# A two-layer mixture-of-experts transformer on one core: keys projected in two halves, with the first half's hats of two chunks traced between them

## The chip, the cores and the metric

One Trainium2 chip, of which the kernel uses one core. The metric is the device time of one launch in microseconds (us), the median over runs. A profiled execution of the kernel before gives the rows below; its own time stands beside the median in the table.

## What is computed

256 latent and 256 context tokens of width 1024 go through two layers, all in fp32. Layer 0 has attention, layer 1 an RWKV-7 mixer; a mixture of 16 experts follows each. The change touches the RWKV mixer alone (16 heads of 64, two scan directions d):

```python
mix = lambda j: h + xx * x_mix[j]
r, k, v = heads(mix(0) @ w_r), heads(mix(2) @ w_k), heads(mix(3) @ w_v)
g = jax.nn.sigmoid(mix(5) @ g1) @ g2
kk = k * heads(k_k)
kk = kk * lax.rsqrt(jnp.maximum(jnp.sum(kk * kk, axis=-1, keepdims=True), 1e-24))
for d in range(2):
    decay = ...   # from mix(1), two small matrices
    iclr = jax.nn.sigmoid(heads(a0[d] + (mix(4) @ a1[d]) @ a2[d]))
    k_d = k * (1.0 + (iclr - 1.0) * heads(k_a))
    ins = (r, decay, k_d, v, -kk, kk * iclr)
    s_ctx, y_c = wkv_scan(zero, *(t[:, :L] for t in ins), reverse=d == 1)
    _, y_l = wkv_scan(s_ctx, *(t[:, L:] for t in ins), reverse=d == 1)
    y = y + jnp.concatenate([y_c, y_l], axis=1)
o = groupnorm(y) + bonus * v
yl = (o * g)[:, L:] @ w_o
```

## The kernel before

One program without branches. Layer 0, then layer 1's mixer (about 980 to 1405 us of the profiled span), its output projection and router, and then layer 1's experts, whose weights stream from HBM. A list scheduler decides at build time in which order the instructions stand on each engine, from the order in which the program traces them, its dependences and its costs; on the chip each engine takes its instructions in that order. Matrix multiplies of the projections run as three fp32r passes on a high and a low part (`mm3`, L148 to L150), for which ScalarE copies the high part of a weight tile (L142) and VectorE, or GpSimd for some, subtracts the low one (L143).

`rwkv` traces the steps of a list, one letter each (L1236): `l` the small matrices of decay and iclr (`loras`), `K` the keys, `R` the receptances, `gate`, `V` the values, `H0` to `H3` the hats of four chunks of 128 tokens, `S0` to `S3` their triangular solves, `c0` to `c7` the sequential scan over pieces of 64 tokens, `M4` to `M7` the outputs.

**Keys.** `proj_k` (L1388) works in four rounds n of 256 columns, four heads each. After each, `k_sink` (L1398) takes the accumulators out as kr and k1 (ScalarE, VectorE), squares kr on GpSimd (L1408), sums the squares by head with TensorE (L1410), raises them to the power -1/2 on GpSimd (`rn`, L1415), transposes the result on TensorE (L1419), copies it to `rT` (VectorE), spreads it over 128 partitions by a product with the constant e4 on TensorE (L1424, fp32), multiplies kr by it (VectorE, L1425) and stores kr and k1 in DRAM (`kks`, issued on ScalarE's queue, L1427). kr and k1 have four buffers each, and the outputs of `R` (`ro`, L1440) and of `V` use the same buffers, as does the gate's sigmoid `gs` (L1543).

**Hats.** `wkv_hat` (L1554) works on pieces: chunk u, direction d, half kh of the heads, 16 pieces in all, four per chunk. A piece loads kk (L1572, from `kks`), sig and icl (L1577, L1579) by SP's queue, multiplies sig by a triangle on TensorE (L1585), takes exponentials on ScalarE (Ep, Em, L1588, L1589), makes A (VectorE, L1594), kk times icl (VectorE, L1608) and BK (GpSimd, L1618), then multiplies them by head in eight small matmuls on TensorE (L1624), four into each of two PSUM tiles, and copies the results to AB on ScalarE (L1630, four copies). 

**Solves.** `wkv_solve` takes the four pieces of a chunk: it begins with a transpose of AB on VectorE (L1651), 62 steps of two VectorE operations (L1658, L1660), and a transpose back (L1662). The scan `c` multiplies the state Z on TensorE and updates it on VectorE (L1837, L1838).

Of the kernel before, what the change touches and what calls it, by code (L numbers as in the profile page):

```python
# [9 lines left out]
F32 = mybir.dt.float32  # L10
# [18 lines left out]
def shape_constants():  # L29
    c = {}  # L30
# [30 lines left out]
    c["gmk"] = np.where(np.arange(128)[:, None] < 64, lt[:, None] > t, lt[:, None] < t)  # L61
    c["e4"] = (i == np.arange(256)[None, :] // 64)
    c["hsel"] = (i // 64 == np.arange(2)[None, :])
# [16 lines left out]
class Net:  # L80
# [1107 lines left out]
    def rwkv(self, st, se, sf):  # L1188
# [46 lines left out]
        self.trit = "k"  # L1235
        for o in ["l", "K", "h", "H0", "R", "H1", "Vm", "gate", "V", "hx", "close", "S0", "H2", "S1", "c0", "H3", "x", "S2", "c1", "S3", "c2", "c3", "M4", "n", "c4", "M5", "c5", "M6", "c6", "M7", "c7", "F"]:  # L1236
            u = int(o[1]) if len(o) == 2 and o[1].isdigit() else None
            if o == "h":
# [19 lines left out]
            elif o == "l":  # L1258
                self.loras(lo, h)
            elif o == "K":  # L1260
                self.proj_k(h)
            elif o == "R":
# [9 lines left out]
            elif o[0] == "H":  # L1272
                q = int("0011"[u])
                self.AB.append(vp[q].tile([128, 2, 16, 64], F32, tag="AB", bufs=2 if q == 0 else 2, name=self.uid("AB")))
                self.wkv_hat(u, self.AB[-1])
            elif o[0] == "S":
# [110 lines left out]

    def proj_k(self, h):  # L1388
        mh, ml = self.mix_split(2, h)
        for n in range(4):  # L1390
            acc = [self.ps(tag="L") for _ in range(2)]
            for k, wh, wl in self.wsplit("rwkv_w_k", n, 256):
                for q in range(2):
                    qs = slice(q * 128, q * 128 + 128)
                    self.mm3(acc[q], wh[:, qs], wl[:, qs], mh[k], ml[k], k == 0, k == KT - 1)
            self.k_sink(n, acc)

    def k_sink(self, n, acc):  # L1398
# [19 lines left out]
        for t in range(4):  # L1418
            nc.tensor.transpose(pt[:, t * 128:(t + 1) * 128], rn[:, t, :], self.ident)  # L1419
        rT = self.lp.tile([4, 512], F32, tag="rT", bufs=2, name=self.uid("rT"))  # L1420
        nc.vector.tensor_copy(rT, pt)
        for i, ts in enumerate(out):
            pb = self.ps(tag="k")
            nc.tensor.matmul(pb, self.cst("e4")[0:4, i * 128:i * 128 + 128], rT, start=True, stop=True)  # L1424
            nc.vector.tensor_tensor(out=ts[0], in0=ts[0], in1=pb, op=ALU.mult)  # L1425
# [127 lines left out]

    def wkv_hat(self, u, AB):  # L1554
        nc = self.nc
        CD = float(np.exp(np.float32(-0.5)))
        lat = u >= 2
        for d in range(2):
# [8 lines left out]
            fm = self.fm[d, u]  # L1567
            for kh in range(2):
                wk = self.hp[(2 * d + kh) % len(self.hp)]
# [49 lines left out]
                nc.sync.dma_start(out=self.hB[d, u][:, :, ks, :], in_=BK)  # L1619
                for lc in range(2):  # L1620
                    p = self.ps((128, 4, 128), tag="G")
                    q64 = slice(64 * d, 64 * d + 64)
                    for q in range(4):
                        nc.tensor.matmul(p[q64, q, :], BK[:, lc, q, Bs] if d == 0 else A[:, lc, q, :],  # L1624
                                         Abd[:, lc, q].rearrange("p a t -> p (a t)"),
                                         start=True, stop=True, skip_group_check=True)
                    pq = p.rearrange("p q (a t) -> p (q a) t", a=2)
                    for jb in range(2):
                        rows = slice(64 * d + 32 * jb, 64 * d + 32 * jb + 32)
                        nc.scalar.activation(AB[rows, lc, 8 * kh:8 * kh + 8, 0:64 - 32 * jb],  # L1630
                                             pq[rows, :, 32 * jb:64], AF.Copy)
                if lat:
# [486 lines left out]
```

## Time and profile before

| | us |
|---|---|
| runs, median of 3 | 1976.08 (1969.65 to 1979.23) |
| the profiled execution, its own time | 1968.82 |
| its span | 1967.0 |
| PE (TensorE) busy in the span | 1703.4 (87%) |
| DVE (VectorE) busy | 972.1 (49%) |
| ACT (ScalarE) busy | 729.0 (37%) |
| POOL (GpSimd) busy | 321.9 (16%) |
| mean granted TensorE clock | 0.936 of 2.4 GHz |

The shares are averages over stages with different limits, so they don't tell what a change in one stage is worth. The rows that matter are those of the stage that the change touches, 1055 to 1410 us, and of the end of the program.

### The profile page before, as it was taken

The numbers are of one execution on the slowest core, as the hardware profiler recorded it, in microseconds if no ns is written. First come the engines' busy times: TensorE is split into PE (matmuls) and PEld (weight loads), VectorE is DVE, ScalarE is ACT, GpSimd is POOL, SyncE is SP. The second block draws the span as 40 slices with busy tenths as digits, with TensorE's granted clock in tenths as the row PEclk, the third lists the DMA queues.
The fourth block names the chain that finished last, engine by engine and source line by source line (L and its number), as shares of the span: only waits on it lengthen the run. The fifth ranks groups of instructions, "written<-read, shape, count | busy, mean of one in ns | idle before, by whom it ended". The sixth has DMA issues, their size and how long they took to land. (4 is left out here: it accounts for less than half of the span.)

```text
span 1967.0 us, 30330 instructions
## 1 busy us (share of the span) xinstructions
PE 1703.4 (87%) x11673; PEld 1037.8 (53%) x11673; DVE 972.1 (49%) x1864; ACT 729.0 (37%) x1379; POOL 321.9 (16%) x313
## 2 busy tenths in 40 slices
PE   5978997889999999994898978889777999988986
PEld 3845565645555555552577767879653333322321
DVE  2466555756555555657745589973653111110101
ACT  2324543545444554543545765642141000100000
POOL 2040032000000000014557353510330000000000
PEclk7989998899999999997898987889988999999999
DMA  8377766699999999995357878635395999999996
GB/s 335 108 295 255 264 186 236 224 356 410 409 410 410 407 409 365 378 361 150 108 186 226 274 209 239 197 102 125 120 392 225 409 409 409 410 408 409 409 409 274
DMA packets 232019, 585.95 MB, mean 298 GB/s; under 512 B 43131, under 2 KB 87443, under 8 KB 231862
## 3 DMA queue, kind: packets, MB, share of 16 engines
q1 hardware_dynamic: 213446, 545.46, 75.2%
q10 hardware_dynamic: 15536, 27.92, 3.9%
q0 software_dynamic: 2880, 10.49, 1.5%
q8 instruction: 96, 1.57, 0.3%
q14 instruction: 61, 0.50, 0.1%
HBM read 544.19 MB, written 39.63 MB: 297 GB/s over the span
## 5 line engine op out<-in xcount | busy, mean ns | idle before, releaser
L143 DVE TENSOR_TENSOR lo<-raw,hi 128x512 fp32r<-128x512 f32 x456 | 305.2, 713 | 208.3 <-ACT hi L142 203.1
L142 ACT ACTIVATE hi<-raw 128x512 fp32r<-128x512 f32 x488 | 292.3, 628 | 215.2 <-PE ps L150 148.1
L1122 PE MATMUL ps<-raw,XT 128*64 128x512 f32 x1024 | 233.5, 597 | 15.3 <-DMA raw<-in_moe_w_dram 15.3
L1122 PEld LDWEIGHTS ps<-raw,XT 128*64 128x64 f32 x1024 | 72.2, 136 | 170.2 <-issue 125.6
L1128 DVE TENSOR_TENSOR h<-h,ps 128x512 f32<-128x512 f32 x16 | 11.0, 688 | 303.9 <-PE ps L1122 303.9
L1140 PE MATMUL ps<-raw,hT 128*64 128x512 f32 x512 | 120.2, 607 | 15.9 <-DVE hT L1133 9.4
L1986 PE MATMUL ps<-raw,XT 128*64 128x512 f32 x512 | 122.7, 600 | 0.0
L148 PE MATMUL ps<-hi,xh 128*128 128x512 f32 x256 | 100.8, 417 | 19.6 <-ACT hi L142 15.6
L149 PE MATMUL ps<-lo,xh 128*128 128x512 f32 x256 | 106.1, 414 | 0.3
L150 PE MATMUL ps<-hi,xl 128*128 128x512 f32 x256 | 102.5, 401 | 0.0
L259 POOL TENSOR_TENSOR rs<-rs,mh 128x2 f32<-128x2 f32 (+2 forms) x5 | 3.9, 772 | 533.9 <-DVE rs L258 533.9
L1140 PEld LDWEIGHTS ps<-raw,hT 128*64 128x64 f32 x512 | 35.2, 138 | 80.4 <-issue 55.2
L1932 POOL DMA_INDIRECT G<-rowbuf,ix x12 | 13.2, 1100 | 392.7 <-DVE oh L1953 261.3
L148 PEld LDWEIGHTS ps<-hi,xh 128*128 128x128 f32 x256 | 49.5, 195 | 48.1 <-ACT hi L142 21.5
L227 PE MATMUL ps<-raw,cv 128*32 128x256 f32 x768 | 61.5, 421 | 9.1 <-DMA raw<-in_ada_w_dram 5.5
L1986 PEld LDWEIGHTS ps<-raw,XT 128*64 128x64 f32 x512 | 34.0, 136 | 64.0 <-issue 61.5
L149 PEld LDWEIGHTS ps<-lo,xh 128*128 128x128 f32 x256 | 49.9, 195 | 24.7 <-DVE lo L143 7.6
L1127 ACT ACTIVATE h<-ps 128x512 f32<-128x512 f32 x16 | 9.6, 597 | 143.0 <-PE ps L1122 143.0
L1144 ACT ACTIVATE ye<-ps 128x512 f32<-128x512 f32 x16 | 9.6, 597 | 141.7 <-PE ps L1140 141.7
L1986 PE MATMUL ps<-raw,hT 128*64 128x512 f32 x256 | 61.3, 600 | 0.8 <-DVE hT L2059 0.8
L148 PE MATMUL ps<-hi,th 128*128 128x512 f32 x128 | 50.0, 407 | 6.2 <-ACT hi L142 6.1
L150 PEld LDWEIGHTS ps<-hi,xl 128*128 128x128 f32 x256 | 49.9, 195 | 9.4
(484 smaller groups left out, 3456.0 us busy)
## 6 DMA issues: line engine op xcount, KB each, us to landing
raw<-in_moe_w_dram SPq DMA_DIRECT2D x384, 1024.0 KB
raw<-in_ada_w_dram SPq DMA_DIRECT2D x48, 1024.0 KB
kk<-kks SPq DMA_DIRECT2D x16, 512.0 KB
hB<-BK SPq DMA_DIRECT2D x16, 512.0 KB
BKm<-hB SPq DMA_DIRECT2D x16, 512.0 KB
raw<-in_attn_w_in_dram SPq DMA_DIRECT2D x6, 1024.0 KB
raw<-in_attn_w_out_dram SPq DMA_DIRECT2D x8, 512.0 KB
ybuf<-ye ACTq DMA_DIRECT2D x8, 512.0 KB
```

The lines of the kernel that those rows point to most:

```text
L142: nc.scalar.activation(hi, src, AF.Copy)
L143: (lo_eng or nc.vector).tensor_tensor(out=lo, in0=src, in1=hi.bitcast(F32), op=ALU.subtract)
L148: mm(out, lh, rh, start=start, stop=False, skip_group_check=True)
L149: mm(out, lh, rl, start=False, stop=False, skip_group_check=True)
L150: mm(out, ll, rh, start=False, stop=stop, skip_group_check=True)
L227: nc.tensor.matmul(p[32 * q:32 * q + 32, :], self.cv[:, k, :], w[:, a, q * 256:(q + 1) * 256], start=(k == 0), stop=(k == KT - 1), skip_gr ...
L1122: nc.tensor.matmul(acc[64 * n:64 * n + 64, :], XT[:, k, e % 4 * 64:e % 4 * 64 + 64], w[:, a, n * 512:(n + 1) * 512], start=(k == 0), stop= ...
L1127: nc.scalar.activation(h, hs[0], AF.Silu)
L1128: nc.vector.tensor_tensor(out=h, in0=h, in1=hs[1], op=ALU.mult)
L1140: nc.tensor.matmul(acc[64 * n:64 * n + 64, :], hT[:, k % 4, (k // 4) * 64:(k // 4) * 64 + 64], w[:, a, n * 512:(n + 1) * 512], start=(k == ...
L1932: nc.gpsimd.indirect_dma_start(out=G, out_offset=None, in_=self.rowbuf[:, :], in_offset=bass.IndirectOffsetOnAxis(ap=idx[:, 0:1], axis=0))
L1986: nc.tensor.matmul(acc[0][64 * n:64 * n + 64, :], lhs(k), w[:, a, ns], start=(k == 0), stop=(k == KT - 1), skip_group_check=True)
```

## The change

Three parts. (1) The list has `K0`, the first two key rounds (heads 0 to 7), then `H00` and `H10`, the first head half of chunks 0 and 1, then `K1`, the last two rounds, then `H01`, `R` and `H11`. Before, `K` stood whole, then `H0`, `R`, `H1`. The solves take whole chunks in both. (2) In `k_sink`, rT is split into a high part (ScalarE copy) and a low part (VectorE subtraction) in one fp32r tile of 36 partitions, and the product with e4 is one fp32r pass of both in place of an fp32 product. (3) In `wkv_hat`, the eight small matmuls of a piece go to one PSUM tile, alternately to its lower and upper 64 partitions.

```diff
@@ -59,7 +59,7 @@
     t = np.arange(64)[None, :]
     c["gm0"], c["gm1"] = lt[:, None] <= t, lt[:, None] >= t
     c["gmk"] = np.where(np.arange(128)[:, None] < 64, lt[:, None] > t, lt[:, None] < t)
-    c["e4"] = (i == np.arange(256)[None, :] // 64)
+    c["e4"] = (i % 32 == np.arange(256)[None, :] // 64) * (i < 64)
     c["hsel"] = (i // 64 == np.arange(2)[None, :])
     late = ("tri0", "tri1", "gm0", "gm1", "gmk", "hsel", "e4")
     off, parts = {}, [[], [], []]
@@ -1233,8 +1233,8 @@
         lo = self.pool(slo, "loras", side="right")
         self.Z, self.main, self.y2, self.late, wk = [None, None], {}, [], [], None
         self.trit = "k"
-        for o in ["l", "K", "h", "H0", "R", "H1", "Vm", "gate", "V", "hx", "close", "S0", "H2", "S1", "c0", "H3", "x", "S2", "c1", "S3", "c2", "c3", "M4", "n", "c4", "M5", "c5", "M6", "c6", "M7", "c7", "F"]:
-            u = int(o[1]) if len(o) == 2 and o[1].isdigit() else None
+        for o in ["l", "K0", "h", "H00", "H10", "K1", "H01", "R", "H11", "Vm", "gate", "V", "hx", "close", "S0", "H2", "S1", "c0", "H3", "x", "S2", "c1", "S3", "c2", "c3", "M4", "n", "c4", "M5", "c5", "M6", "c6", "M7", "c7", "F"]:
+            u = int(o[1]) if o[1:].isdigit() else None
             if o == "h":
                 slo.close()
                 vp.append(self.pool(ssv, "solve", side="right"))
@@ -1257,8 +1257,8 @@
                 self.hat_tiles("A", wk)
             elif o == "l":
                 self.loras(lo, h)
-            elif o == "K":
-                self.proj_k(h)
+            elif o[0] == "K":
+                self.proj_k(h, (2 * u, 2 * u + 1))
             elif o == "R":
                 self.proj_r(h)
             elif o == "V":
@@ -1271,8 +1271,9 @@
                 self.gate_hidden(h)
             elif o[0] == "H":
                 q = int("0011"[u])
-                self.AB.append(vp[q].tile([128, 2, 16, 64], F32, tag="AB", bufs=2 if q == 0 else 2, name=self.uid("AB")))
-                self.wkv_hat(u, self.AB[-1])
+                if u == len(self.AB):
+                    self.AB.append(vp[q].tile([128, 2, 16, 64], F32, tag="AB", bufs=2, name=self.uid("AB")))
+                self.wkv_hat(u, self.AB[u], (0, 1) if len(o) == 2 else (int(o[2]),))
             elif o[0] == "S":
                 self.wkv_solve(vp[int("0101"[u])], u, self.AB[u])
             elif o == "x":
@@ -1385,9 +1386,21 @@
                     ws = slice(b * width, (b + 1) * width)
                     yield m * c + a + b, wh[:, ws], wl[:, ws]
 
-    def proj_k(self, h):
-        mh, ml = self.mix_split(2, h)
-        for n in range(4):
+    def proj_k(self, h, ns):
+        if ns[0]:
+            return self.proj_k_part(ns)
+        nc = self.nc
+        self.mk = self.mix_split(2, h)
+        self.e4 = self.lp.tile([36, 256], F32R, name="e4r")
+        nc.scalar.activation(self.e4, self.cst("e4")[0:36, :], AF.Copy)
+        self.rT = [self.lp.tile([36, 512], F32R, name=f"rT{i}") for i in range(2)]
+        for t in self.rT:
+            nc.gpsimd.memset(t.bitcast(F32), 0.0)
+        self.proj_k_part(ns)
+
+    def proj_k_part(self, ns):
+        mh, ml = self.mk
+        for n in ns:
             acc = [self.ps(tag="L") for _ in range(2)]
             for k, wh, wl in self.wsplit("rwkv_w_k", n, 256):
                 for q in range(2):
@@ -1417,11 +1430,12 @@
         pt = self.ps((4, 512), tag="k")
         for t in range(4):
             nc.tensor.transpose(pt[:, t * 128:(t + 1) * 128], rn[:, t, :], self.ident)
-        rT = self.lp.tile([4, 512], F32, tag="rT", bufs=2, name=self.uid("rT"))
-        nc.vector.tensor_copy(rT, pt)
+        rT = self.rT[n % 2]
+        nc.scalar.activation(rT[0:4, :], pt, AF.Copy)
+        nc.vector.tensor_tensor(out=rT[32:36, :], in0=pt, in1=rT[0:4, :].bitcast(F32), op=ALU.subtract)
         for i, ts in enumerate(out):
             pb = self.ps(tag="k")
-            nc.tensor.matmul(pb, self.cst("e4")[0:4, i * 128:i * 128 + 128], rT, start=True, stop=True)
+            nc.tensor.matmul(pb, self.e4[:, i * 128:i * 128 + 128], rT, start=True, stop=True)
             nc.vector.tensor_tensor(out=ts[0], in0=ts[0], in1=pb, op=ALU.mult)
             for a, t in enumerate(ts):
                 nc.scalar.dma_start(out=self.kks[:, a, 2 * n + i], in_=t.rearrange("p (v t) -> p v t", v=2))
@@ -1551,7 +1565,7 @@
     Bs = {0: slice(0, 64), 1: slice(64, 128)}
     Ks = {0: slice(64, 128), 1: slice(0, 64)}
 
-    def wkv_hat(self, u, AB):
+    def wkv_hat(self, u, AB, khs):
         nc = self.nc
         CD = float(np.exp(np.float32(-0.5)))
         lat = u >= 2
@@ -1565,7 +1579,7 @@
             mid, end = (0, 64) if d == 0 else (64, 0)
             v4 = lambda t: t.rearrange("p k (c t) -> p k c t", c=2)
             fm = self.fm[d, u]
-            for kh in range(2):
+            for kh in khs:
                 wk = self.hp[(2 * d + kh) % len(self.hp)]
                 ks = slice(4 * kh, 4 * kh + 4)
                 kk = self.ht(wk, "kk", [128, 2, 4, 128])
@@ -1617,18 +1631,18 @@
                 nc.vector.tensor_tensor(out=kd, in0=kd, in1=icl, op=ALU.mult)
                 nc.gpsimd.tensor_tensor(out=bk(Ks), in0=v4(kd), in1=Em[:, :, :, inc], op=ALU.mult)
                 nc.sync.dma_start(out=self.hB[d, u][:, :, ks, :], in_=BK)
-                for lc in range(2):
-                    p = self.ps((128, 4, 128), tag="G")
-                    q64 = slice(64 * d, 64 * d + 64)
-                    for q in range(4):
-                        nc.tensor.matmul(p[q64, q, :], BK[:, lc, q, Bs] if d == 0 else A[:, lc, q, :],
+                p = self.ps((128, 4, 128), tag="G")
+                for q in range(4):
+                    for lc in range(2):
+                        nc.tensor.matmul(p[64 * lc:64 * lc + 64, q, :], BK[:, lc, q, Bs] if d == 0 else A[:, lc, q, :],
                                          Abd[:, lc, q].rearrange("p a t -> p (a t)"),
                                          start=True, stop=True, skip_group_check=True)
-                    pq = p.rearrange("p q (a t) -> p (q a) t", a=2)
+                pq = p.rearrange("p q (a t) -> p (q a) t", a=2)
+                for lc in range(2):
                     for jb in range(2):
                         rows = slice(64 * d + 32 * jb, 64 * d + 32 * jb + 32)
                         nc.scalar.activation(AB[rows, lc, 8 * kh:8 * kh + 8, 0:64 - 32 * jb],
-                                             pq[rows, :, 32 * jb:64], AF.Copy)
+                                             pq[64 * lc + 32 * jb:64 * lc + 32 * jb + 32, :, 32 * jb:64], AF.Copy)
                 if lat:
                     nc.gpsimd.tensor_tensor(out=rr, in0=kd, in1=rr, op=ALU.mult)
                     pbn = self.ps((128, 8), tag="G")
```

Lines past `k_sink` stand 14 lower in the code after the change (L1424 is L1438 there, L1618 is L1632). Only the RWKV stage's order differs; from the tail of the scan to the end the instructions stand alike.

GpSimd's queue before, from the squares of key round 3 on (ksq), with rn2172 the power of round 2 and rn2196 that of round 3; the first hat's rows follow behind these:

```order
L1408 TENSOR_TENSOR ksq2192_9234<-kr2190_9232 128x512
L1408 TENSOR_TENSOR ksq2195_9244<-kr2193_9242 128x512
L1415 TENSOR_TENSOR rn2172_9141<-rn2172_9141,mh_66 128x16
L143 TENSOR_TENSOR lo2286_9615<-raw2282_9596,hi2285_9614 128x512
L143 TENSOR_TENSOR lo2291_9649<-raw2287_9630,hi2290_9648 128x512
L143 TENSOR_TENSOR lo2300_9691<-raw2296_9672,hi2299_9690 128x512
L1321 MEMSET Abd_9279 128x1024
L1652 MEMSET T2463_10447 128x1024
L1653 MEMSET T2463_10447 128x32
L1415 TENSOR_TENSOR rn2196_9252<-rn2196_9252,mh_66 128x16
L143 TENSOR_TENSOR lo2305_9725<-raw2301_9706,hi2304_9724 128x512
```

The same queue now, with BK2170, BK2181 and BK2191 the second to fourth hat piece's, ksq2231 and ksq2234 the squares of round 3:

```order
L1632 TENSOR_TENSOR BK2170_9137<-kk2162_9114,Em2166_9121 128x4x2x64
L1605 COPY fm01_8367<-Em2177_9170 128x4x2
L1604 COPY fm11_8371<-Ep2186_9217 128x4x2
L1632 TENSOR_TENSOR BK2181_9186<-kk2173_9163,Em2177_9170 128x4x2x64
L1605 COPY fm11_8371<-Em2187_9218 128x4x2
L1421 TENSOR_TENSOR ksq2231_9443<-kr2229_9441 128x512
L1421 TENSOR_TENSOR ksq2234_9453<-kr2232_9451 128x512
L1632 TENSOR_TENSOR BK2191_9234<-kk2183_9211,Em2187_9218 128x4x2x64
L1428 TENSOR_TENSOR rn2212_9350<-rn2212_9350,mh_66 128x16
L1428 TENSOR_TENSOR rn2235_9461<-rn2235_9461,mh_66 128x16
L143 TENSOR_TENSOR lo2404_10166<-raw2400_10147,hi2403_10165 128x512
```

Both powers stood ahead of the first hat piece; now both stand behind the fourth piece's BK.

ScalarE's queue before, around the last store of key round 3 (kr2193) and the first hat's exponentials; ro2316 is an output of R:

```order
L1427 DMA kks_8324<-kr2193_9242 128x512 [waits DMAHW0_49,DVE_49]
L1370 ACTIVATE mxh2368_10016<-mx2384_10047 128x512 [waits DVE_49,PE_49]
L142 ACTIVATE hi2408_10117<-raw2407_10115 128x512 [waits DMAHW6_49,Pool_49]
L1588 ACT_TABLE_LOAD [waits DMAHW5_49]
L1588 ACTIVATE Ep2205_9288<-ps2207_9290 128x260 [waits PE_49]
L1589 ACTIVATE Em2206_9289<-ps2207_9290 128x260
L1588 ACTIVATE Ep2205_9288<-ps2208_9295 128x260 [waits PE_49]
L1589 ACTIVATE Em2206_9289<-ps2208_9295 128x260
L142 ACTIVATE hi2410_10133<-raw2407_10115 128x512 [waits PE_49,Activation_49]
L1370 ACTIVATE mxh2369_10017<-mx2385_10051 128x512 [waits DVE_49,PE_49]
L1441 ACTIVATE ro2316_9808<-ps2294_9670 128x512 [waits PE_49]
```

ScalarE's queue now, behind the last of the early hats' copies; kr2206 and kr2209 are key round 2's, ro2305 and ro2329 outputs of R, gs2387 the gate's sigmoid, kr2229 round 3's, hi2403 and what follows weights of V:

```order
L1434 ACTIVATE rT0_8830<-ps2213_9353 4x512 [waits PE_49]
L1441 DMA kks_8324<-kr2206_9330 128x512 [waits DMAHW5_49,DVE_49]
L1441 DMA kks_8324<-kr2209_9340 128x512 [waits DMAHW6_49,DVE_49]
L1455 ACTIVATE ro2305_9763<-ps2283_9625 128x512 [waits DMAHW5_49]
L1456 DMA rsc_8331<-ro2305_9763 128x512 [waits DMAHW7_49,Activation_49]
L1455 ACTIVATE ro2329_9907<-ps2307_9769 128x512 [waits DMAHW6_49]
L1456 DMA rsc_8331<-ro2329_9907 128x512 [waits Activation_49]
L1557 ACT_TABLE_LOAD
L1557 ACTIVATE gs2387_10095<-ps2375_10057 128x160 [waits DMAHW7_49]
L1434 ACTIVATE rT1_8831<-ps2236_9464 4x512 [waits PE_49]
L142 ACTIVATE hi2403_10165<-raw2400_10147 128x512 [waits PE_49]
```

The waits on a DMAHW semaphore are for transfers. Before, round 3's store stood ahead of the first hat; now the last outputs of R, the gate's sigmoid and V's next weights stand behind round 2's stores, and ro2305 and ro2329 wait for transfers.

TensorE's queue now; ps2192 is the fourth early piece's product, ps2213 the transposes of round 2, ps2388 and ps2390 the gate's, ps2391 the first of V:

```order
L1637 MATMUL ps2192_9246<-Abd_9063,A2190_9231 64x128 x8
L1432 MATMUL ps2213_9353<-C_60,rn2212_9350 4x128 x4
L1438 MATMUL ps2214_9360<-rT0_8830,e4r_8828 128x512
L1438 MATMUL ps2215_9365<-rT0_8830,e4r_8828 128x512
L1423 MATMUL ps2228_9440<-C1_8332,ksq2231_9443 128x2 x4
L1423 MATMUL ps2228_9440<-C1_8332,ksq2234_9453 128x2 x4
L1559 MATMUL ps2388_10097<-C_60,gs2387_10095 128x128
L1560 MATMUL ps2388_10097<-C_60,gs2387_10095 32x128
L1559 MATMUL ps2390_10104<-C_60,gs2389_10102 128x128
L1560 MATMUL ps2390_10104<-C_60,gs2389_10102 32x128
L148 MATMUL ps2391_10109<-hi2396_10115,mxh2351_10009 128x512
```

Before, rounds 2 and 3's products with e4 (L1424) stood ahead of the first hat's triangle, and the gate's transposes stood between hat pieces. Now round 2's stand behind the fourth early piece, ahead of the gate and V, and round 3's transposes and e4 products (L1432, L1438) stand 21 and 41 rows behind V's first row.

## Rows read from the trace of the kernel before

**Rows 1.** The page: TensorE's busy tenths and GB/s in 40 slices of 49.2 us.
```profile
PE   5978997889999999994898978889777999988986
...
GB/s 335 108 295 255 264 186 236 224 356 410 409 410 410 407 409 365 378 361 150 108 186 226 274 209 239 197 102 125 120 392 225 409 409 409 410 408 409 409 409 274
```

**Rows 2.** The chain of waits, its first expert matmul and a late transfer: start, us, what.
```profile
1493.29 1.07 PE ps L1122 x3
...
1889.59 18.55 DMA raw<-in_moe_w_dram
```

**Rows 3.** Busy time by stage: PE, PEld, DVE, ACT, POOL, clock, DMA, rate.
```profile
971.00:975.00 4.00, 4.00 (x13) 3.09 (x12) 1.68 (x3) 0.93 (x2) 1.47 (x2) 0.57 0.42 168
1055.00:1093.00 38.00, 29.44 (x200) 25.71 (x198) 26.51 (x31) 25.74 (x52) 29.15 (x24) 0.91 0.77 240
1093.00:1154.40 61.40, 61.33 (x330) 50.12 (x328) 44.15 (x77) 42.66 (x94) 21.36 (x25) 1.00 0.79 243
1120.30:1268.90 148.60, 126.61 (x1537) 109.56 (x1536) 136.81 (x261) 104.55 (x217) 68.94 (x83) 0.83 0.78 220
```

**Rows 4.** Timeline, SP's queue: loads of the first and third hat piece.
```profile
1055.76 0.72 SPq L1577 DMA_DIRECT2D sig<-sgs  x1
...
1088.23 2.91 SPq L1572 DMA_DIRECT2D kk<-kks  x2
...
1094.21 0.42 SPq L1579 DMA_DIRECT2D icl<-ics  x1
```

**Rows 5.** Timeline, TensorE: the first triangle, a key sink's e4 product, a hat's.
```profile
1065.12 1.98 PE L1424 MATMUL ps<-rT,C 4*128 4x512 f32 x4
...
1070.12 0.71 PE L1585 MATMUL ps<-C,sig 128*128 128x130 f32 x4 [0.55 <-DVE kr L1425]
...
1097.23 1.96 PE L1624 MATMUL ps<-Abd,BK 128*64 128x128 f32 x16
```

**Rows 6.** Timeline, GpSimd: round 3's power; the first, third and fourth piece's BK.
```profile
1058.44 2.91 POOL L1415 TENSOR_TENSOR rn<-rn,mh 128x16 f32<-128x16 f32 x1 [1.37 <-DVE rn L1414]
...
1083.45 1.18 POOL L1618 TENSOR_TENSOR BK<-kk,Em 128x512 f32<-128x512 f32 x1 [1.02 <-DVE kk L1617]
...
1105.62 1.18 POOL L1618 TENSOR_TENSOR BK<-kk,Em 128x512 f32<-128x512 f32 x1
...
1112.93 1.20 POOL L1618 TENSOR_TENSOR BK<-kk,Em 128x512 f32<-128x512 f32 x1 [3.10 <-DVE kk L1617]
```

**Rows 7.** Timeline, ScalarE: round 3's last store, an output of R, the gate's sigmoid.
```profile
1070.69 0.86 ACTq L1427 DMA_DIRECT2D kks<-kr  x1
...
1077.07 0.62 ACT L1441 ACTIVATE ro<-ps 128x512 f32<-128x512 f32 x1
...
1092.16 0.50 ACT L1543 ACTIVATE gs<-ps 128x160 f32<-128x160 f32 x2
```

**Rows 8.** Timeline, TensorE: V's first row, and two that follow on each other.
```profile
1092.93 0.47 PE L148 MATMUL ps<-hi,mxh 128*128 128x512 f32 x1
...
1093.47 0.40 PE L150 MATMUL ps<-hi,mxl 128*128 128x512 f32 x1
1093.71 0.40 PE L148 MATMUL ps<-hi,mxh 128*128 128x512 f32 x1
```

**Rows 9.** Timeline, VectorE: the third piece, the first solve, a state update of the scan.
```profile
1094.76 0.69 DVE L1594 TENSOR_TENSOR A<-kk,Ep 128x512 f32<-128x512 f32 x1 [0.89 <-DMA kk<-kks]
...
1101.34 0.69 DVE L1608 SCALAR_TENSOR_TENSOR kk<-icl,kk 128x512 f32<-128x512 f32 x1 [5.89 <-DMA icl<-ics]
...
1120.27 2.02 DVE L1651 STREAM_TRANSPOSE S<-AB 128x1024 f32<-128x1024 f32 x1
...
1268.90 0.68 DVE L1838 TENSOR_TENSOR Z<-Z,F 128x512 f32<-128x512 f32 x1
```

**Rows 10.** Timeline, TensorE: the same 128x512 pass at a lower clock.
```profile
972.33 0.63 PE L148 MATMUL ps<-mxh,hi 128*128 128x512 f32 x1
972.76 0.63 PE L149 MATMUL ps<-mxl,hi 128*128 128x512 f32 x1
```

## Prediction

> **What bounds the kernel now.** I read the page first. Its slices [rows 1] show the last fifth of the span at 409 GB/s with TensorE eight or nine tenths busy: there the experts' weights stream. The chain of waits [rows 2] says the same from the other side: its last fifth is transfers of `raw<-in_moe_w`, and the chain comes to them through the layer's first expert matmuls at 1493.29. So the end is a stream that cannot begin in earnest before layer 1's mixer and router are through (the slices from 1278 to 1426 us move 102 to 125 GB/s). Whatever moves the end of the mixer moves the end of the program by the same amount, and I read the rest of the price inside the mixer.
>
> The stage table [rows 3] then tells what limits each part of it. From 1055 to 1093 no engine is full (TensorE 29.4 of 38 us). From 1093 to 1154 TensorE is full (61.33 of 61.40): V's projection with hats between. From the first solve at 1120 to the second state of the scan at 1269 VectorE is busy 136.8 of 148.6 us, 92%.
>
> **The change part by part.**
>
> *The new order.* It lets the first hat piece start earlier, which is its gain. Before, the first triangle ran at 1070.12 and waited for VectorE's multiply of the last key sink, which held a PSUM bank [rows 5]. Its sig had been on the way since 1055.76 [rows 4]. A load of kk was issued at 1088.23 and used at 1094.76 [rows 4, 9], so it lands within 6.5 us; 1055.76 + 6.4 = 1062.2 is when the triangle can run now. Gain at this point: 8 us.
>
> What stands behind it is the loss. The order shows that rounds 2 and 3 of the key sink are now queued behind all four early pieces, on three engines: their powers on GpSimd behind the fourth BK, their transposes and e4 products on TensorE behind the fourth piece's products, their stores on ScalarE behind the fourth piece's copies. And behind round 2's stores stand, on ScalarE, the last two outputs of R (which reuse kr and k1), the gate's sigmoid and V's further weight splits; on TensorE the gate's transposes and all of V. I follow that chain with durations of the trace:
>
> 1. The fourth BK. Before, from the first triangle to the fourth BK it took 1112.93 - 1070.12 = 42.8 us [rows 5, 6]. The same from 1062.2 gives 1105.0. With the shortest pitch seen (1105.62 to 1112.93, 7.3 us) three times behind the first piece's 13.3 it is 35.2 us and 1097.4. I take 42.8, since the waits in it are for loads and buffers, which stay.
> 2. Round 2's power starts when that BK is done, 1105.0 + 1.2 = 1106.2, and takes 2.9 [rows 6]. Round 3's follows at once.
> 3. From a power's start to the last store's issue took 1058.44 to 1070.69 = 12.2 us before [rows 6, 7], amid R's matmuls. TensorE has little to do here now, and the e4 product is one pass. I take 8: 1114.2. The ends are 6.6 and 12.2.
> 4. The first R output waits for that store to land, is copied (0.6 [rows 7]), stored, and the sigmoid's buffer waits for that store. Two landings. A landing lies between 3.6 us (kk, from the end of its 2.9 us issue) and 7.1 (icl, issued 1094.21, used 1101.34) [rows 4, 9]; I take 5. From the sigmoid's start to V's first row it is 0.8 as before, 1092.16 to 1092.93 [rows 7, 8]. V's first row: 1114.2 + 5 + 0.6 + 5 + 0.8 = 1126, against 1092.93 [rows 8]: 33 us later.
> 5. Round 3's e4 product stands 41 rows behind that, at 0.24 us a row of V [rows 8]: 9.8 us, 1135.8. The pass, a multiply of about 0.69 and an issue like the 0.86 of [rows 7] make 1.9, then come store and load, two landings of 5: the third piece of chunk 0 (the first of `H01`) has its kk at 1147.5. Before, its place was 1094.76 [rows 9].
> 6. Two pieces remain before the first solve. Before, from the third piece's A to the first solve was 1120.27 - 1094.76 = 25.5, of which 5.9 was a late icl [rows 9]; 19.6 remains. First solve: 1167.1, against 1120.27. **+46.8 us.**
>
> From there the delay is carried on. VectorE was 92% busy up to the scan [rows 3], so it cannot catch up by more than its holes. Chunk 1 has its first half ready by then, so two pieces fewer lie behind the first solve: six VectorE instructions each of about 0.69 [rows 9], some 8 us. On the other side V's weight subtractions and V's end (192 passes at 0.24 us are 46 us, with a piece or two between 50, so 1176 against 1154 [rows 3]) are still to come, with H11, in the same stretch. I let the two cancel: 0, with ends -8 and +12 (the whole of VectorE's idle time there).
>
> *One pass for e4.* Four products of 1.98 us [rows 5]. By the 128x512 fp32r pass, 0.39 to 0.47 for each of two [rows 8], 0.8 is left: 4 x 1.2 = 5 us of TensorE at most. Two of the four fall in rounds 0 and 1, the other two in my step 3 and 5, which count them. ScalarE's copy of four rows takes the place of VectorE's, and VectorE's subtraction that of the copy. The two memsets and the copy of e4 come once, early. Sum: within 2 us, taken as 0 beyond the steps above; if the cover (TensorE waiting in rounds 2 and 3) were gone, a gain of 5.
>
> *Eight matmuls in two halves of one tile.* A piece's sixteen passes took 1.96 us [rows 5]. If the two halves do not overlap, nothing changes; if they do, half is saved. Only the third and fourth piece of chunk 0 lie on the path to the first solve: 0 to -2 us. The others are hidden, where TensorE waits for hats (29.4 of 38 us busy) or VectorE sets the pace. In V's full stretch the saving is worth about 1 us per piece, which the later start of V swallows. I take 0. The Trainium skill, "TensorEngine Tiling (Array Packing)", section "Theoretical Speedup", gives up to 2 times where one dimension is 64 or less: by it the 16 pieces would save 16 x 0.98 = 15.7 us of TensorE, and the sum would be lower by the 2 us on the path alone. No row here shows this form.
>
> **Sum.** +46.8 us on the profiled execution's 1968.82, so 2015.6 for it. The median of the runs is 7.3 higher, 1976.08, and the forecast is made for that: 1976.1 + 46.8 = **2023 us**.
>
> **The rivals.**
>
> *Larger: the clock falls too.* TensorE gets little to do between R's end and 1126. The trace has a stretch at a granted clock of 0.57 of 2.4 GHz [rows 3], so near the 1.2 GHz level, where a pass took 0.43 us from start to start [rows 10] against 0.24. If V's 192 passes ran at that rate throughout, 192 x 0.19 = 36 us more: 2059. It decides if the granted clock is under 0.6 from V's start to its end. Against it: V fed without gaps ran at 1.00 [rows 3]. The Trainium skill, "TensorE: Matmul & The Clock Gate", section "HAM oscillation", says that an engine waiting for transfers falls back to the low clock; the 0.57 stretch agrees that there is such a level, and a low start of V, not all of V, is what I expect of it.
>
> *No change: the delay is caught.* If pieces run at the shortest pitch (-7.6), the sinks at 6.6 (-1.4) and four landings at 3.6 (-5.6), the first solve is 32 us late. VectorE could take back its 12 us of holes and 8 us of moved pieces, and TensorE's savings in e4 and hats another 5 or so: about +7 us, 1983. For it speaks that two pieces of chunk 1 are done early; against it that all has to go right at once.
>
> *Faster: the sinks are not held.* If the early pieces passed so fast that round 2's power came by 1073 (1092.9 less the 20 us of steps 2 to 4), V would begin where it did, with the first piece 8 us earlier and its full stretch 5 us shorter by the hats' and e4's saved passes: -13, 1963. The point that decides is the fourth BK before 1072, 10 us behind the first triangle. The trace has 42.8 us there and no pitch under 7.3, so this needs a queue other than the one that the order shows.
>
> That the change does not do what it says can hold for the two halves only (no overlap); it is priced above at 0 to 2 us and changes no case.
>
> **How the numbers follow.** The forecast, a first solve held by 24 to 65 us: 0.80. The clock on top: 0.08. Caught: 0.07. Faster: 0.05. A measurement of this kernel tells about 0.5% (10 us) from no change, its three runs lying 9.6 us apart. Slower by more than that: 0.80 + 0.08 = 0.88; the same: 0.07; faster: 0.05. The range takes the bounds of the sum: low, -7.6 - 1.4 - 5.6 - 8 - 2 on 46.8, +22, 1998; high, +4.2 for the sinks, 4 x 2.1 for landings, +12 carried and a third of the clock's 36, +83, 2059. The ends will not all fall together on the high side, so I stop at 2056. What is left out is the two small cases and half of the clock's.
>
> **What would show it.** In the profile of the changed kernel: the first triangle near 1062; round 2's power right behind the fourth BK, near 1106; the R outputs' copy waiting on a transfer of kr; the first row of V near 1126, its last near 1176; the first solve's transpose near 1167; the scan at the same pitch, and the first expert matmul near 1540. In the stage table TensorE should be far less busy between 1075 and 1125 than the 29.4 of 38 before. The forecast is wrong if V starts by 1100, or if the first solve is late by 40 us and the scan's first states are not. If the pieces of the hats show 1.96 us again, the two halves do not overlap.

## The result, and the profile after

The changed kernel takes 2002.69 us (median of 4 runs, 1999.18 to 2006.64) against 1977.65 for the kernel before beside it (4 runs, 1969.65 to 1980.44): **1.0134 times as long, 95% interval 1.0098 to 1.017**, 25 us by the medians. Its profiled execution took 2006.64 us with a span of 2004.9, 37.8 us more than the profiled one of before.

The timeline of the changed kernel, first GpSimd (start us, us, engine, line, operation, idle before and its releaser). It answers to [rows 6]:

```profile
1085.51 1.18 POOL L1632 TENSOR_TENSOR BK<-kk,Em 128x512 f32<-128x512 f32 x1 [0.17 <-POOL fm L1604]
...
1103.99 1.18 POOL L1632 TENSOR_TENSOR BK<-kk,Em 128x512 f32<-128x512 f32 x1 [0.68 <-DVE rn L1427]
1105.12 2.91 POOL L1428 TENSOR_TENSOR rn<-rn,mh 128x16 f32<-128x16 f32 x1
1115.93 2.90 POOL L1428 TENSOR_TENSOR rn<-rn,mh 128x16 f32<-128x16 f32 x1 [7.89 <-DVE rn L1427]
```

The fourth early piece's BK ends at 1105.2 and the power of key round 2 starts at once. GpSimd was only the last of the engines that held it: its input, VectorE's `rn`, came at 1103.78, right ahead of this BK, and that had waited for TensorE's sums of the squares of round 2. The squares were made by 1020.2; the sums stand behind the third early piece's passes in TensorE's queue and ran at 1098.61 (both rows below). ScalarE, against [rows 7]:

```profile
1112.04 0.93 ACTq L1441 DMA_DIRECT2D kks<-kr  x2
1114.10 0.60 ACT L1455 ACTIVATE ro<-ps 128x512 f32<-128x512 f32 x1 [4.37 <-DMA kks<-kr]
...
1117.37 0.30 ACT L1557 ACTIVATE gs<-ps 128x160 f32<-128x160 f32 x1
```

R's output waits 4.37 us for the store of the keys, the sigmoid behind it. TensorE, against [rows 5, 8]:

```profile
1064.19 1.13 PE L1599 MATMUL ps<-C,sig 128*128 128x130 f32 x8 [3.42 <-DMA sig<-sgs]
...
1086.05 1.09 PE L1637 MATMUL ps<-Abd,A 128*64 128x128 f32 x16 [0.36 <-ACT Abd L1626]
...
1096.71 1.97 PE L1637 MATMUL ps<-Abd,BK 128*64 128x128 f32 x16 [5.34 <-DVE BK L1623]
1098.61 3.57 PE L1423 MATMUL ps<-C,ksq 128*128 128x2 f32 x16
...
1118.49 0.78 PE L148 MATMUL ps<-hi,mxh 128*128 128x512 f32 x1
...
1119.49 0.63 PE L150 MATMUL ps<-hi,mxl 128*128 128x512 f32 x1
1119.92 0.63 PE L148 MATMUL ps<-hi,mxh 128*128 128x512 f32 x1
...
1130.69 0.73 PE L1438 MATMUL ps<-rT,e4r 36*128 36x512 f32 x2
```

V starts at 1118.49 in place of 1092.93, its first rows 0.43 us apart. VectorE, against [rows 9]:

```profile
1103.78 0.16 DVE L1427 TENSOR_SCALAR rn<-ps 128x16 f32<-128x16 f32 x1
...
1109.76 0.68 DVE L1435 TENSOR_TENSOR rT<-ps,rT 4x512 fp32r<-4x512 f32 x1 [5.82 <-ACT rT L1434]
...
1127.06 0.68 DVE L1435 TENSOR_TENSOR rT<-ps,rT 4x512 fp32r<-4x512 f32 x1 [7.70 <-ACT rT L1434]
...
1141.20 0.69 DVE L1608 TENSOR_TENSOR A<-kk,Ep 128x512 f32<-128x512 f32 x1 [6.29 <-DMA kk<-kks]
...
1163.31 2.03 DVE L1665 STREAM_TRANSPOSE S<-AB 128x1024 f32<-128x1024 f32 x1
...
1314.98 0.68 DVE L1852 TENSOR_TENSOR Z<-Z,F 128x512 f32<-128x512 f32 x1
```

The third piece of chunk 0 starts at 1141.20 in place of 1094.76, the first solve at 1163.31 in place of 1120.27, the scan's first update (c1) at 1314.98 in place of 1268.90. The chain of waits has its first expert matmul 37.8 us later, as [rows 2] had it at 1493.29:

```profile
1531.13 13.95 PE ps L1122 x64
```

Where the time went is plainest in the stage tables, of before and then of the change (columns: stretch, us, busy PE, PEld, DVE, ACT, POOL with instruction counts, granted clock, DMA share, GB/s). The last stretch ends with the scan's last state update, 1388.5 and 1427.25:

```profile
1062.00:1100.00 38.00, 29.44 (x181) 24.63 (x179) 27.20 (x33) 25.90 (x53) 24.26 (x21) 0.91 0.79 242
1100.00:1140.00 40.00, 40.00 (x221) 32.95 (x220) 28.79 (x45) 29.95 (x66) 17.51 (x19) 1.00 0.86 270
1140.00:1180.00 40.00, 28.34 (x214) 23.18 (x213) 34.93 (x67) 29.31 (x59) 19.80 (x25) 0.86 0.78 204
1062.00:1388.50 326.50, 284.00 (x4312) 250.94 (x4310) 247.52 (x442) 187.98 (x369) 121.35 (x139) 0.89 0.68 190
```

```profile
1062.00:1100.00 38.00, 23.41 (x151) 21.16 (x151) 25.75 (x28) 27.52 (x57) 20.90 (x22) 0.73 0.83 267
1100.00:1140.00 40.00, 32.24 (x141) 25.70 (x141) 9.25 (x16) 15.10 (x29) 13.27 (x10) 0.70 0.33 112
1140.00:1180.00 40.00, 35.10 (x208) 27.74 (x206) 29.25 (x48) 27.63 (x60) 13.14 (x15) 1.00 0.74 229
1062.00:1427.25 365.25, 294.47 (x4324) 258.82 (x4325) 245.08 (x444) 189.87 (x367) 121.98 (x141) 0.80 0.61 172
```

VectorE does the same work in both, 247.5 and 245.1 us. What grew is its holes: 326.5 - 247.5 = 79.0 and 365.25 - 245.1 = 120.2, 41 us more. 20 of these lie between 1100 and 1140, where it is busy 9.25 us in place of 28.79. The window ends with the scan's last update, so with the same work the sum of the holes follows the end of the mixer by construction; it tells where the time went, not why.

### The profile page after: what moved, and what is told of

It reads as the page before. It is cut to its first block, busy times and chain, and to the rows that moved or that the text cites. A ratio compares the mean times of both kernels' runs of the same rounds, so it can differ in the third digit from the quotient of the medians.

```text
span 2004.9 us, 30301 instructions
## 1 busy us (share of the span) xinstructions
PE 1710.9 (85%) x11665; PEld 1046.1 (52%) x11665; DVE 969.7 (48%) x1864; ACT 734.8 (37%) x1386; POOL 318.4 (16%) x315
## 5 line engine op out<-in xcount | busy, mean ns | idle before, releaser
L148 PE MATMUL ps<-hi,xh 128*128 128x512 f32 x256 | 101.8, 421 | 19.6 <-ACT hi L142 15.5
L148 PEld LDWEIGHTS ps<-hi,xh 128*128 128x128 f32 x256 | 50.3, 198 | 48.6 <-ACT hi L142 21.8
```

The costliest lines, as they stand in the source:

```text
L148: mm(out, lh, rh, start=start, stop=False, skip_group_check=True)
```

## The experiments

Each was timed against the kernel before on the same chip. The theory: the loss comes from the place of the key sinks in the engines' queues. The first rival: it comes from the new forms of the e4 product and of the hats. The lists below are the part of the order list between `l` and `Vm`.

**Both new forms in the old order.**

```diff
-"K0", "h", "H00", "H10", "K1", "H01", "R", "H11"
+"K0", "K1", "h", "H0", "R", "H1"
```

> The order of before (keys whole, then H0, R, H1) with both new forms, the one-pass e4 product and the hats' two halves. Theory (the loss is the key sinks' place in the queues): no loss, the time within -14 to +2 us of before; V's first row near 1090, the first solve near 1117; a piece's sixteen hat passes at 1.1 us where they took 1.96. Rival (the new forms cost, by stalls between the two halves or ScalarE's extra copies): slower by 15 to 30 us here too.

Measured: 1957.89 us, 0.9907 times before (0.9883 to 0.9931). The rival falls: the forms gain 18.5 us, 4.5 more than the expected range has. The first solve is at 1121.18, V at 1091.32; three of the first four pieces' hat passes take 1.09 us:

```profile
1087.50 1.09 PE L1637 MATMUL ps<-Abd,BK 128*64 128x128 f32 x16
...
1121.18 2.04 DVE L1665 STREAM_TRANSPOSE S<-AB 128x1024 f32<-128x1024 f32 x1 [0.52 <-ACT AB L1644]
...
1229.50 0.68 DVE L1852 TENSOR_TENSOR Z<-Z,F 128x512 f32<-128x512 f32 x1
...
1062.00:1373.87 311.87, 269.33 (x4286) 236.37 (x4285) 240.81 (x439) 184.66 (x364) 117.43 (x137) 0.89 0.70 198
```

VectorE's holes are 311.9 - 240.8 = 71.1 us.

**The new order with both old forms:** the change's parts in `k_sink` and `wkv_hat` undone, its list kept.

```diff
-        rT = self.rT[n % 2]
-        nc.scalar.activation(rT[0:4, :], pt, AF.Copy)
-        nc.vector.tensor_tensor(out=rT[32:36, :], in0=pt, in1=rT[0:4, :].bitcast(F32), op=ALU.subtract)
+        rT = self.lp.tile([4, 512], F32, tag="rT", bufs=2, name=self.uid("rT"))
+        nc.vector.tensor_copy(rT, pt)
...
+                for lc in range(2):
+                    p = self.ps((128, 4, 128), tag="G")
+                    q64 = slice(64 * d, 64 * d + 64)
```

> The new order with both old forms. Theory: as slow as the change or some us more, +25 to +40 us on before; round 2's power right behind the fourth BK at 1104 to 1108, V's first row at 1118 to 1124, the first solve at 1163 to 1170. Rival (the new forms cost): back to before within 6 us.

Measured: 2010.03 us, 1.0167 (1.0141 to 1.0192); first solve at 1167.84. The order alone makes the loss. One expectation was missed: round 2's power runs ahead of the fourth BK here, not behind it, and the loss is as large.

```profile
1108.98 3.37 POOL L1423 TENSOR_TENSOR rn<-rn,mh 128x16 f32<-128x16 f32 x1
1112.29 1.19 POOL L1626 TENSOR_TENSOR BK<-kk,Em 128x512 f32<-128x512 f32 x1
```

The sums of round 2 stand behind the third early piece on TensorE here too (at 1104.32), so the hold does not depend on GpSimd's order. V starts at 1125.02, 1 us past the expected range. Against the change's 1.0134 the new forms take back some 7 us by the medians, with intervals that overlap, and not 18.5.

**The keys first, the hats still interleaved.**

```diff
-"K0", "h", "H00", "H10", "K1", "H01", "R", "H11"
+"K0", "K1", "h", "H00", "H10", "H01", "R", "H11"
```

> Both key halves ahead of all hats, the rest of the new order (H00, H10, H01, R, H11) and both new forms kept. Theory: the sinks are through before the first hat, so V's first row is back at 1085 to 1095; what is left is that the first solve now waits for six pieces in place of four, two pieces of 7 to 11 us, so it comes at 1132 to 1142; time 0 to +15 us on before. Rival (the interleaving of two chunks by halves makes the loss by itself, wherever the sinks stand): first solve at 1155 or later, time +20 us or more.

Measured: 1988.38 us, 1.0065 (1.0045 to 1.0086). V at 1090.29, the first solve at 1138.03, as expected:

```profile
1138.03 2.03 DVE L1665 STREAM_TRANSPOSE S<-AB 128x1024 f32<-128x1024 f32 x1
...
1062.00:1405.12 343.12, 276.39 (x4285) 243.04 (x4284) 236.72 (x439) 186.09 (x363) 117.70 (x137) 0.84 0.63 180
```

The new order without any hold costs 30 us on both forms in the old order, though only 17 in the first solve. It is a second cost, which the prediction had not set apart. Two things are still together in it: the pieces of two chunks alternate, and a chunk's pieces come by halves of the heads, where `H0` takes one direction after the other. The run with chunk 0's halves together, further below, parts them. Against the change, which differs in the place of the last two key rounds alone, the kernel is 14 us faster and the first solve 25 us earlier: that is what the hold costs.

**One chunk's pieces between the key halves.**

```diff
-"K0", "h", "H00", "H10", "K1", "H01", "R", "H11"
+"K0", "h", "H00", "K1", "H01", "R", "H10", "H11"
```

> H00 alone between the key halves, then H01, R, H10, H11: two early pieces in place of four, and the first solve needs four pieces again; new forms kept. Theory (what counts is how many pieces the sinks stand behind): round 2's power behind the second BK, near 1087, V's first row near 1100, the third piece's A near 1122, the first solve near 1142, so a bit over half of the change's delay of it; time +8 to +22 us on before. Rival (any cut of the keys costs the full hold, by the stores' landing): first solve at 1158 or later, +25 us or more.

Measured: 1990.40 us, 1.0074 (1.0048 to 1.01). Round 2's power comes at 1080.75 behind the second BK, V at 1094.19, the third piece's BK at 1119.92, the first solve at 1137.39. With two pieces ahead in place of four the power comes 24 us sooner. The kernel is 32 us slower than both forms in the old order, and the change is 45 slower; but here too the pieces come by halves, so the 32 us are not the hold alone.

**Buffers of their own for R's outputs and the gate's sigmoid**, otherwise the change:

```diff
-                o = self.lp.tile([128, 2, 256], F32, tag=("kr", "k1")[i], bufs=4, name=self.uid("ro"))
+                o = self.lp.tile([128, 2, 256], F32, tag="ro", bufs=1, name=self.uid("ro"))
...
-            gs = self.lp.tile([128, 160], F32, tag=("kr", "k1")[t], bufs=4, name=self.uid("gs"))
+            gs = self.lp.tile([128, 160], F32, tag="gs", bufs=2, name=self.uid("gs"))
```

> The change, with a buffer of their own for R's outputs and two for the gate's sigmoid, so that neither waits for the key stores; the key sinks stand behind the fourth piece as before, on ScalarE even behind V's first outputs. It parts the two holds: V free, the keys of heads 8 to 15 held. Theory A (the first solve is what counts): V's first row at 1085 to 1100, the third piece of chunk 0 still at 1135 to 1155, the first solve at 1155 to 1175, time within 12 us of the change's (+15 to +40 on before). Theory B (the late V is what counts): time back to +10 us on before or less.

Measured: 2008.11 us, 1.016 (1.0137 to 1.0183).

```profile
1084.57 0.48 PE L148 MATMUL ps<-hi,mxh 128*128 128x512 f32 x1
...
1108.13 2.91 POOL L1428 TENSOR_TENSOR rn<-rn,mh 128x16 f32<-128x16 f32 x1
...
1159.51 1.92 DVE L1665 STREAM_TRANSPOSE S<-AB 128x1024 f32<-128x1024 f32 x1 [0.48 <-ACT AB L1644]
```

V is 34 us earlier than in the change and the time no better. So the late V costs nothing by itself. Theory A holds: with V free, the late keys of heads 8 to 15 still hold the first solve at 1159.51, and the loss stays. That these late keys cost time is shown by the run with the keys first, 14 us faster than the change.

**The hats' two halves alone, old order:** the list as in the first run, `k_sink` as before.

```diff
-            nc.tensor.matmul(pb, self.e4[:, i * 128:i * 128 + 128], rT, start=True, stop=True)
+            nc.tensor.matmul(pb, self.cst("e4")[0:4, i * 128:i * 128 + 128], rT, start=True, stop=True)
```

> The order of before with the hats' two halves alone (old e4 product). The run of both forms was 18.5 us faster than before, with the first solve in its old place and the first update of the scan's second step at 1229 in place of 1269, because VectorE's queue has it ahead of most of the third solve. Theory (VectorE's queue order makes that gain): here the update stands later in the queue than with both forms, about a third of the way from there to its old place, so the gain is smaller: -4 to -14 us on before. Rival (the shorter matmuls themselves make it): 16 pieces at 0.87 us, -12 to -18 us here, and none with e4 alone.

**The one-pass e4 product alone, old order:** the list as in the first run, `wkv_hat`'s matmuls as before.

```diff
-                        nc.tensor.matmul(p[64 * lc:64 * lc + 64, q, :], BK[:, lc, q, Bs] if d == 0 else A[:, lc, q, :],
+                        nc.tensor.matmul(p[q64, q, :], BK[:, lc, q, Bs] if d == 0 else A[:, lc, q, :],
```

> The order of before with the one-pass e4 product alone (old hats). VectorE's queue has the scan's second update as early as with both forms. Theory (queue order): -8 to -18 us on before, the update near 1230. Rival (the shorter matmuls): 5 us of TensorE at most, -5 to 0.

Measured: 1968.77 us, 0.9949 (0.9928 to 0.9969), and 1971.76 us, 0.9974 (0.9957 to 0.9991): about 10 and 5 us, of the 18.5 together; the theory's -8 to -18 us for e4 alone is missed. With e4 alone the scan's first update is at 1227.07, as early as with both, and the gain is still only 5: the idea that this one update's place makes the gain falls. Sizes fit shorter matmuls (16 x 0.87 = 14 us at most, and 5), but the next but one run shows that the order of the pieces moves the time by as much, so what part each has stays open.

**One chunk's pieces early, then the other chunk's.**

```diff
-"K0", "h", "H00", "H10", "K1", "H01", "R", "H11"
+"K0", "h", "H00", "K1", "H10", "H01", "R", "H11"
```

> H00 alone between the key halves, then H10, H01, R, H11. Against the run with one chunk's pieces (H00, keys, H01) the sinks stand behind the same two pieces, but the first solve needs six pieces. Theory (hold by the sinks, and two pieces of 8 to 10 us each): V's first row near 1094 as there, the first solve 14 to 20 us later than its 1137, at 1151 to 1158; time +14 to +28 us on before, between that run and the change. Rival (order of the pieces doesn't matter): first solve within 5 us of 1137.

Measured: 1987.76 us, 1.0057 (1.0038 to 1.0076). The first solve is at 1156.96, 20 us behind that of the run with one chunk, as expected, and the time is no worse: a miss. Nor is it worse than with the keys first (1.0065), where the pieces stand in the same order and the first solve comes 19 us sooner. The second solve's start gives the reason in part: 1176.77 here, 1190.32 there. With both chunks half done, both solves come close together, and VectorE's holes up to the last update are 109.1 and 114.3 us (343.9 - 234.8 and 347.7 - 233.4). So the first solve's start alone does not give the time; what else does is not shown by this run.

**Keys first, chunk 0's halves together.**

```diff
-"K0", "h", "H00", "H10", "K1", "H01", "R", "H11"
+"K0", "K1", "h", "H00", "H01", "R", "H10", "H11"
```

> Keys whole, then chunk 0's four pieces by halves (H00, H01), R, chunk 1's (H10, H11), new forms. Against the run with the keys first and H00, H10, H01 (12 us slower than before) only chunk 1's first half moves behind chunk 0's second. Theory (with the keys' hold gone, what was left was that the first solve stood behind six pieces in place of four): the first solve back at 1118 to 1126, VectorE's holes from 1062 to the last state update back to 70 to 80 us from 106, time -20 to -8 us on before, as with both forms in the old order. Rival (tracing the hats by halves of the heads costs by itself, in loads or in the order of R): +5 us on before or more.

Measured: 1975.36 us, 1.0002 (0.9986 to 1.0018). The first solve is back, at 1118.71, but the gain isn't; the expected time and the expected 70 to 80 us of holes were missed, and the time lies under the rival's 5 us on before as well:

```profile
1118.71 2.02 DVE L1665 STREAM_TRANSPOSE S<-AB 128x1024 f32<-128x1024 f32 x1
...
1275.74 0.69 DVE L1852 TENSOR_TENSOR Z<-Z,F 128x512 f32<-128x512 f32 x1
...
1062.00:1395.77 333.77, 278.88 (x4300) 246.21 (x4299) 245.65 (x440) 188.20 (x368) 119.24 (x138) 0.84 0.67 187
```

This order differs from both forms in the old order in one thing: the four pieces of chunks 0 and 1 come by halves of the heads, not one direction after the other. The instructions are the same. The solves of chunks 0 and 1 start and end within 3.2 us of those of both forms in the old order, and yet the scan's first update comes 46 us later and the kernel is 17.5 us slower, with 88.1 us of holes against 71.1.

VectorE's built order differs. A solve has 62 rows there (31 steps of two operations, not 62 steps). All 62 of the third solve stand ahead of the scan's first update here, as in the kernel before; with both forms in the old order 3 do. That is a likely cause, not a shown one: with e4 alone none stands ahead, and the gain is 5 us. TensorE's granted clock up to the last update is lower here too, 0.84 against 0.89, and no run sets either by hand.

This run is the base for the other orders that trace by halves, and it parts the 45 us between both forms in the old order and the change: some 18 us for tracing by halves of the heads (0.9907 to 1.0002), 12 for alternating two chunks with the keys first (to 1.0065), 14 for the hold behind four pieces (to 1.0134). The hold behind two pieces of one chunk costs 14 as well (1.0002 to 1.0074); in the run before this one it costs nothing against the run with the keys first (1.0065 to 1.0057). Each of these differences is uncertain by 5 us or more, as their intervals show.

**Both chunks' hats ahead of R.**

```diff
-"K0", "h", "H00", "H10", "K1", "H01", "R", "H11"
+"K0", "K1", "h", "H0", "H1", "R"
```

> Keys whole, then both chunks' hats, then R, new forms: a try for a version faster than both forms in the old order (18.5 us faster than before). Theory: R isn't needed by the first two chunks, but nothing else waits for the hats earlier than the first solve either, and the scheduler puts R's matmuls where TensorE is free: within 5 us of that version, -24 to -13 us on before. Rival (R's later outputs hold the third chunk's hats): -13 us or worse.

Measured: 1956.36 us, 0.9897 (0.9871 to 0.9923), the same within the intervals as both forms in the old order. VectorE's solves and state updates stand at the very same rows of its built order in the two. Either one is faster than the kernel before and than the change.

## Why the prediction was right, and where its sizes were off

The sign held, and so did the chain of steps up to the first solve. 2002.69 lies in the range of 1998 to 2056, near its lower end; the forecast of 2023 is 20 us too high. The cause that the prediction names, the held key sinks, is there, but the runs make it one of three.

- **The early hats.** First triangle 1062.2 forecast, 1064.19 measured; fourth BK 1105.0 and 1103.99; round 2's power 1106.2 and 1105.12. The 42.8 us from triangle to BK became 39.8. The step puts round 2's wait on GpSimd behind this BK; the trace has it on TensorE first, behind the third piece (sums at 1098.61). With nothing ahead of it on GpSimd the power could have started 1.2 us sooner at most, so the time came out right; in the run with both old forms it did start ahead of this BK.
- **The sink's tail.** From power to store 8 forecast, 6.9 measured (1105.12 to 1112.04).
- **The landings** were mis-sized. I took 5 us for each from rows of loads; the wait of R's output ended 2.1 us after the store's issue, and the sigmoid waited for no transfer that the trace shows. V started at 1118.49, not 1126. As the run with own buffers shows, this term did not bear on the time.
- **Round 3.** Its power did not follow at once but 7.89 us later, behind VectorE's `rn`, which waits for the sums of round 3 on TensorE (from 1112.07); these stand behind round 2's e4 product, as TensorE's order on record shows. It cost nothing, since the product stands behind V's rows anyway. These took 12.2 us in place of 9.8, as V began at the lower clock: here the rival of the clock showed itself, for some ten rows 0.43 us apart (granted clock 0.50, so 1.2 GHz, from 1118.5 to 1123.5) against 0.24 later (1.00 from 1124 to 1130). The e4 product came at 1130.69 (1135.8 forecast), the third piece at 1141.20 (1147.5), then 22.1 us to the first solve (19.6).
- **The first solve:** +46.8 forecast, +43.0 measured.
- **The carry:** 0 forecast; the first expert matmul is 37.8 us later, so 5 us were caught, within the bounds of -8 and +12. That looks like a delay passed on nearly whole, but it isn't: without the hold the first solve is 25 us earlier and the kernel only 14 us faster, and with the keys first and chunk 0's halves together the first solve is in its old place and the kernel 18 us slower than both forms in the old order. That the carry came out near 0 is in part luck, since costs that the prediction had not seen stood in for what was caught.
- **The term that was furthest off** is the last, "the median of the runs is 7.3 higher, and the forecast is made for that". It takes the difference of two profiled executions for that of two medians. The profiled ones differ by 37.8 us, the medians by 25.0: that of before lies 8.8 under its median of this comparison (and under every other run of before on record, the lowest at 1969.07), that of the change 4.0 over. Of the 21.8 us between +46.8 and +25.0, 12.8 are of this kind, 3.8 are the first solve's and 5.2 the carry's.
- **New forms.** "Sum: within 2 us" for e4 and 0 for the hats do not hold in the old order, where they are worth 18.5 us; in the new order they are worth about 7 together by the medians. So the order alone cost 34 us (the run with both old forms) where 46.8 were forecast, and the forms took 7 of it back. The passes of a piece went from 1.96 to 1.09 us at full clock. The Trainium skill, "TensorEngine Tiling (Array Packing)", section "Theoretical Speedup", has up to 2 times for a dimension of 64 or less; the trace shows 1.8.
- **The rivals.** Faster and caught did not come. Against "caught" the holes speak: between 1100 and 1140 VectorE stood idle at the sinks' rows of its queue (two waits of 5.82 and 7.70 us for `rT`), with later work behind them. The clock fell for longer than V's start: it was 0.70 from the first solve to the scan's first update, against 0.83 before; that stage took 151.7 us against 148.6, so there it cost little.

What the prediction did not see is that the loss has three parts. It took the six pieces ahead of the first solve as part of the hold; the run with the keys first shows that the new order without the hold costs twice what the hold does (30 and 14 us). And of these 30 some 18 come with the order of the pieces within a chunk, which moves the first solve not at all; through what they cost stays open.

## What to carry to other kernels

Work that is pulled forward in the traced order pulls its queue rows ahead of what it has displaced on every engine: before splitting a producer to start consumers early, follow the displaced producer's last steps through each engine's queue to the first thing that waits for them all. A partial result gained nothing here, where the stage behind takes whole chunks. The start of a single step can mislead by 20 us; and since the order of the pieces alone moved the time by 18 us, compare orders that differ in one thing only.

## What the runs showed of the hardware

- A store of 256 KB from ScalarE's queue let its buffer go within 2.1 us of its issue (1112.04 to 1114.10; DMA share 0.59), where a 512 KB load of kk took up to 6.5 [rows 4, 9] (DMA share 1.03 from 1088 to 1095).
- Sixteen 64-column passes into alternate halves of one PSUM tile took 1.09 us at a granted clock of 1.00 (1086.05), and 1.97 at 0.50 (1096.71). The old form, sixteen passes in two tiles, took 1.96 at 1.00 [rows 5].
